# SP's queue as a fourth engine in the list that orders a hybrid-attention layer, with every transposing issue a step of its own

## The chip, the core and the metric

The kernel runs on one core of a Trainium2 chip. The metric is device time in microseconds (us): the median of several executions. The engines are called PE (matrix multiply), ACT (ScalarE), DVE (VectorE), POOL (GpSimd) and SP (SyncE, which here only issues DMAs). Every engine works through its own instructions in order. SP's instructions are DMA issues; one that waits for a semaphore holds those behind it.

## The reference

One layer, 512 tokens (`SEQ`), width 2048 (`D_MODEL`), three token mixers of 4 heads of 128, all in float32:

```python
hn = rmsnorm(x, norm_g)
proj = jnp.einsum('bsd,dc->bsc', hn, w_in)
br = proj[..., :QKVG_COLS].reshape(b, s, N_BRANCH, 4, BRANCH_W)      # q, k, v, g of three branches
f_logit = proj[..., QKVG_COLS:QKVG_COLS + N_HEADS] + b_f
gates = jax.nn.sigmoid(proj[..., QKVG_COLS + N_HEADS:] + b_gate).reshape(b, s, N_BRANCH, D_MODEL)
ya = forgetting_attention(qa, ka, va, f_logit)        # A: softmax with a cumulative forget bias, causal
yb = chunked_relpos_attention(qb, kb, vb, rel_bias)   # B: chunks of 64 and a learned relative bias
yc = stick_breaking_attention(qc, kc, vc)             # C: stick-breaking weights in log space
ys = jnp.stack([from_heads(ya), from_heads(yb), from_heads(yc)], axis=2)
ys = ys * jax.nn.silu(br[:, :, :, 3])
up = jnp.einsum('bsnw,nwd->bsnd', ys, w_up)
merged = jnp.sum(gates * up, axis=2)
return x + jnp.einsum('bsd,de->bse', merged, w_out)
```

The input projection makes 2048 -> 12,292 columns: 6,144 for q, k, v, g, 4 forget logits, and 6,144 merge gates.

## The kernel before

Float32 products are made on PE from two float32r parts each: a value is split into a high part (ACT, L249) and a low part (DVE, L253), and three products are summed (the low-low product is left out). Two columns of 128 are computed as one pair with seven products in place of eight (Strassen-Winograd), so a pair of columns is seven units. A unit has a weight tile `raw` of 512 KB, its split `w`, and 16 matmuls (L268): eight of 512 columns for the high part and eight of 256 for the low one. PE accumulates a unit in a PSUM bank; ACT (L786, L790, L807, L840) or DVE takes it out.

The order of units is written in `HEADS`: after the first head, which is computed while x is loaded, each further head brings a pair of its q and k, and the letters say what follows: `s` a pair of two heads' g, `g` a pair of merge-gate columns (24 such pairs in all, taken from one row of gates), `v` the value projection of the next branch (14 units). Between a unit's matmuls the steps of the heads are put in: norms, scores, softmax or stick-breaking, the transposing of the weights, the product with v, SiLU. Then come the `up` units (12 heads' outputs, 16 column blocks, with the gates) and the `out` units with the residual.

What comes when is settled before the chip runs, by a list: a small discrete-event plan (`Flow`). Every piece of work is a generator that yields either something to wait for (an `Event` with a planned time, free buffers in `Slots`) or `(engine, microseconds)`. The plan always takes next the step that can start first, of equal ones that with the earlier due time (ready time plus a slack: 0 for weight loads, 5 or 3 for a head's steps), and moves that engine's clock. The instruction is emitted when its step is taken. PE, ACT and DVE execute in the order of this plan (`manual_schedule`). SP's queue is not an engine of the plan: a transfer is emitted when its generator gets to it, `landing` estimates when its data are there, and only the first 48 transfers (`N_FIRST`) and those of the values are pinned to the order of emission (`keep_in_program_order`). The others may be put in another order when the program is built.

Transfers on SP: weights (`raw`), x, `xn`, fetches of what was put into DRAM (`g`, `vr`, `yr`, `sg`, `tb`, `cb`), stores (`gl` gates, `gd` a second head's g, `vd` values, `yd` heads' outputs), and transposes. Those take a head's weights of 512 x 512, causal, as ten blocks of 128 x 128: for every row block i, ACT lays the words' two halves apart (`apart`, L1230), then i + 1 transposing issues go out (L1234), and when all ten have landed, ACT puts the halves together (`together`, L1244). Before, the plan emits the i + 1 issues at once and reckons their landing aside:

```python
            turned[0] = max(turned[0], flow.fin + 0.3) + 1.3 * (i + 1)
            self.event("x", i).t = turned[0] + XLATE
```

The last head has its weights transposed on PE (`soft_trans`). The second summand of a unit's weights is added by POOL's queue (`add_up`, L286).

Of the kernel before, what the change touches and what calls it, by code (L numbers as in the profile page):

```python
# [16 lines left out]
P = 128  # L17
# [20 lines left out]
PE, ACT, DVE = 0, 1, 2  # L38
# [26 lines left out]
class Flow:  # L65
# [98 lines left out]
def hybrid_kernel(  # L164
# [106 lines left out]
    line = [0.0, 0.0]  # L271

    def landing(ready, kb):

        line[0] = max(line[0], ready) + 0.5
        line[1] = max(line[1], line[0] + 1.0) + kb / (340.0 if line[1] < 60.0 else 370.0)
        return line[1] + 1.5

    def fetch(to, src, ready, kb, queue=nc.sync, pinned=False):
        i = queue.dma_start(to, src)  # L280
        if pinned or len(first) < N_FIRST and queue is nc.sync:
            first.append(tc.keep_in_program_order(i))
        return Event(landing(ready, kb))

    def add_up(to, src, ready, kb, pinned=False):
        i = nc.gpsimd.dma_start(to, src, accum_op=ALU.add)  # L286
        if pinned:
            tc.keep_in_program_order(i)
        line[1] = max(line[1], ready + 1.0) + kb / 170.0
        return Event(line[1] + 2.5)  # L290
# [10 lines left out]
    first = [tc.keep_in_program_order(nc.sync.dma_start(begin_in, begin))]  # L301
# [76 lines left out]
    def load_unit(u):  # L378
        if isinstance(u, (Pair, VUnit)):
            if u is u.task.units[0]:  # L380
                yield from u.task.load()
            return
        for s in u.srcs:
            yield raws, 1
            t = raw_tile(u.shape)
            u.raw = t
            u.there.t = fetch(t, s, flow.ready, 4 * u.shape[0] * P * P // 1024, nc.scalar if u is units[0] else nc.sync).t
# [215 lines left out]
    class PairTask:  # L603
# [9 lines left out]
        def __init__(self, src1, src2, ops, c1_done=None, c2r_done=None, c2_done=None, late=False, rest=None,  # L613
                     x1_first=False, plain_end=False):
            self.plain_end = plain_end
            self.src, self.ops, self.late, self.rest = (*src1, *src2), ops, late, rest
            self.done = {"c1": c1_done, "c2r": c2r_done, "c2": c2_done}
            self.order = (1, 5, 2, 3, 6, 7, 4) if late else (1, 2, 6, 5, 7, 3, 4)
            if x1_first:
                self.order = (1, 5, 6, 2, 7, 3, 4)  # L620
            self.w, self.there, self.ps = {}, {p: Event() for p in range(1, 8)}, {}
            self.ev = {p: Event() for p in range(1, 8)}
            self.r, self.r_ev, self.c2_ev = None, Event(), Event()
            self.bank, self.pools, self.tile = {}, accs, acc
            self.units = [Pair(self, i) for i in range(7)]
# [4 lines left out]
        def load(self):  # L630
            a11, a12, a21, a22 = self.src
            for p, srcs in ((5, (a21, a22)), (1, (a11,)), (2, (a12,)), (7, (a11, a21)), (4, (a22,))):
                yield raws, 1
                t = self.w[p] = raw_tile()
                ev = fetch(t, srcs[0], flow.ready, 512)
# [71 lines left out]
        def after_of(self, i):  # L707
# [68 lines left out]
            def go():  # L776
# [31 lines left out]
                elif p == 7:  # L808
# [10 lines left out]
                    yield from fold(self.c2[:, RH], self.v)  # L819
                    give(t2s)  # L820
# [10 lines left out]
                else:  # L831
# [11 lines left out]
                    give(bank)  # L843
                    finished("c2", self.c2)
# [27 lines left out]
    class ValueTask:  # L872
# [19 lines left out]
        def keep(self, g, s):  # L892

            def go(c):
                yield rstd_ev
                for i, h in enumerate((LH, RH)):
                    yield ACT, act_us(HS)
                    nc.scalar.activation(c[:, h], c[:, h], AF.Copy, scale=rcol[:, 2 * i + s:2 * i + s + 1])
                nc.sync.dma_start(self.dram[g][s], c)
                t = landing(flow.fin, 256)  # L900
                t2s.free.append(t)
                self.kept[g][s].t = t
            return go
# [4 lines left out]
        def load(self):  # L908
# [3 lines left out]
            def begin(p, kh, queue):  # L912
# [6 lines left out]
                for to, c in pieces(p, kh):  # L919
                    ev = fetch(to, src({5: 2, 1: 0, 2: 1, 7: 0, 4: 3}[p], kh)[:, c], flow.ready,  # L920
                               128 * (c.stop - c.start), queue, True)
# [93 lines left out]
    def forget_bias():  # L1015
# [6 lines left out]
        nc.sync.dma_start(parts, fd.rearrange("(n h) (c t) -> n (h c) t", h=NH, t=T).rearrange("n c t -> c n t"))  # L1022
# [23 lines left out]
        nc.sync.dma_start(fd2.rearrange("h (c t) -> (h c) t", t=T), v)  # L1046
# [11 lines left out]
    turned = [0.0]  # L1058

    class Head:  # L1060
# [93 lines left out]
        def soft_start(self):  # L1154
# [3 lines left out]
            if n == A:  # L1158
                yield f2_ev
                self.bias = t2("cb")  # L1160
                nc.sync.dma_start(self.bias, fd2[self.h:self.h + 1, :].partition_broadcast(P))
                yield Event(landing(flow.now, 256))
# [4 lines left out]
            else:  # L1167
                self.bias = t2("tb")
                ev = fetch(self.bias, rel[self.h], flow.now, 256)
# [44 lines left out]
        def apart(self, i):  # L1214
# [18 lines left out]
            for j in range(i + 1):  # L1233
                nc.sync.dma_start_transpose(out=self.tt[j][:, :, (i - j) * P:(i - j + 1) * P],  # L1234
                                            in_=u[:, 2 * j * P:2 * (j + 1) * P])
# [76 lines left out]
        def value(self):  # L1312
# [9 lines left out]
            for s in range(2):  # L1322
                ev = fetch(to[:, :, s, :], task.dram[g][s].rearrange("p (i h d) -> p i h d", i=2, h=2)[:, :, d, :],
                           flow.now, 128)
# [6 lines left out]
        def silu(self):  # L1331

            if (self.n, self.h) in gd:
# [4 lines left out]
                yield fetch(g, d, flow.now, 256)  # L1338
# [22 lines left out]
        def av(self):  # L1361
# [48 lines left out]
    def spill(n, d, c):  # L1410
        gl[n, d] = dp.tile([P, S], F32, name=nm("gl"))
        nc.sync.dma_start(gl[n, d], c)
        stored(t2s, 1, 256)

    def gate_units(late=False, x1_first=False):
        n, d = gates.pop(0)

        def keep(i):
            def go(c):
                yield from by_norm(c)  # L1420
                spill(n, d + i, c)
# [4 lines left out]
    def far(n, h):  # L1426
# [3 lines left out]
        def go(c):  # L1430
            yield from by_norm(c)
            nc.sync.dma_start(d, c)
            ev.t = landing(flow.fin, 256)
# [3 lines left out]
    def first_quad(head):  # L1437
# [57 lines left out]
        def take_f():  # L1495
# [5 lines left out]
            for j in range(NQ):  # L1501
                nc.sync.dma_start(fd[NH * j:NH * (j + 1), :], v[32 * j:32 * j + NH, :])
# [67 lines left out]
    def split_y(i):  # L1570
        def go():
# [4 lines left out]
            else:  # L1576
                yield t2s, 1
                t = t2("yr")
                yield fetch(t, yd[n, h], flow.now, 256)
# [11 lines left out]
    def gates_of(d):  # L1591
        evs = []
        for n in (C, B, A):
            yield t2s, 1
            sig[n, d] = t2("sg")
            evs.append(fetch(sig[n, d], gl[n, d], flow.now, 256))
# [115 lines left out]
    def out_pair(e):  # L1712
# [3 lines left out]
        def rest(task):  # L1716
            yield t2s, 2
            for i in range(2):
                r[i] = t2("xr")
                ev = fetch(r[i], xT[e + i], flow.now, 256)  # L1720
# [35 lines left out]
    def loads():  # L1756
        def x(kt):
# [5 lines left out]
            x_in[kt].t = fetch(xraw[kt], xT[kt], 0.0, 256).t  # L1763

        def n(i):
            yield t2s, 1
            t = t2("xn")
            n_in[i].t = fetch(t, xn[i // NQ, i % NQ], 0.0, 256).t
# [44 lines left out]
    line[:] = 0.8, 1.9  # L1813
# [29 lines left out]
N_FIRST = 48  # L1843
# [53 lines left out]
```

## Time and profile before

| | |
|---|---|
| median of 3 runs | 1307.88 us (1307.13 to 1309.7) |
| the profiled execution's own time | 1307.3 us |
| its span, first to last instruction | 1305.6 us |
| mean granted PE clock | 0.999 |
| busy: PE, PE weight load, DVE, ACT | 1294.0, 1128.8, 1144.7, 883.8 us |
| transposing issues on SP | 110 |

The profile is of one execution. Rows of busy time by stretch read: the stretch in us from the start and its length, then for PE, PE's weight load, DVE, ACT and POOL the busy us with the number of instructions, then the granted PE clock (1.00 is full), the mean busy share of the 16 DMA engines and GB/s. Rows of waits read: engine, tile and line that waited, what ended the wait; us in total, times, the longest. Rows of the timeline read: start, length, engine, line, operation, out<-in, count, and in brackets how long the engine had been idle and what ended it; neighbours of one kind are merged, so a length on SP (SPq) runs from the first issue's start to the last one's end. A PE row that is merged takes in small pauses.

### The profile page before, as it was taken

Reading aid. Unit: us, or ns where it says so; the run is one execution under the profiler, and the core shown is the slowest. Engines: PE = TensorE matmul, PEld = TensorE weight load, DVE = VectorE, ACT = ScalarE, POOL = GpSimd, SP = SyncE. Lnnn points to the kernel's source line nnn. Section 1 sums busy time; section 2 is a strip of 40 time slices with the busy share of each in tenths; the row PEclk is TensorE's granted clock in tenths of the full one; section 3 lists DMA queues with packets and bytes.
Section 4 is the critical chain, followed back from the end, with each engine's and each line's share of the span. In section 5 each row is a group of like instructions: output and inputs, shape, how many; then the busy total and the mean of one; then the engine's idle time right before and its main releaser. Section 6 shows DMA issues by size and latency. Waiting matters only on the chain.

```text
span 1305.6 us, 20205 instructions
## 1 busy us (share of the span) xinstructions
PE 1294.0 (99%) x7247; PEld 1128.8 (86%) x7247; DVE 1144.7 (88%) x1693; ACT 883.8 (68%) x1380; POOL 106.8 (8%) x138
## 2 busy tenths in 40 slices
PE   9999999999999999999999999999999999999998
PEld 6888888888888888888888888888888888898887
DVE  8989989888898999989869989999898888898786
ACT  8887677767867768667767767776857655454443
POOL 0200100020010000101100001001010000001000
PEclk9999999999999999999999999999999999999999
DMA  9879797878789878886888669898789765778883
GB/s 340 238 190 253 175 237 203 219 201 209 219 211 225 227 201 218 211 236 174 213 217 218 183 184 256 180 254 195 214 224 298 259 194 169 205 180 251 236 239 110
DMA packets 132420, 282.90 MB, mean 217 GB/s; under 512 B 43344, under 2 KB 51536, under 8 KB 132320
## 3 DMA queue, kind: packets, MB, share of 16 engines
q1 hardware_dynamic: 111200, 217.32, 52.1%
q0 software_dynamic: 17376, 59.78, 26.8%
q10 hardware_dynamic: 3744, 4.52, 1.0%
q8 instruction: 57, 0.93, 0.3%
q14 instruction: 43, 0.35, 0.1%
HBM read 249.92 MB, written 24.42 MB: 210 GB/s over the span
## 4 chain that ended last, share of the span: by engine, by line
PE 85%; DVE 5%; DMA 5%; ACT 3%; issue 1%; SPq 0%; ACTq 0%; POOL 0%; DVEq 0%; POOLq 0%
PE acc L268 71%; PE att L268 10%; DMA raw<-in_w_col 3%; DVE w L253 2%; ACT w L249 1%; DMA raw<-in_w_v 1%; PE att L264 1%; PE att L265 1%; PE att L263 1%; PE att L1372 1%; PE att L1373 1%; PE att L1371 0%; DMA g<-gd 0%; SPq L1234 0%; ACT p L1244 0%
## 5 line engine op out<-in xcount | busy, mean ns | idle before, releaser
L253 DVE TENSOR_TENSOR w<-raw,w 128x1024 fp32r<-128x1024 f32 (+2 forms) x424 | 499.8, 1184 | 109.4 <-ACT w L249 107.7
L249 ACT ACTIVATE w<-raw 128x1024 fp32r<-128x1024 f32 (+2 forms) x424 | 434.5, 1026 | 212.2 <-PE acc L268 84.5
L268 PE MATMUL acc<-x,w 128*128 128x512 f32 (+1 forms) x2656 | 500.1, 339 | 1.6 <-ACT v L790 1.0
L268 PEld LDWEIGHTS acc<-x,w 128*128 128x128 f32 x2656 | 425.1, 190 | 68.2 <-issue 3.0
L268 PE MATMUL acc<-t,w 128*128 128x256 f32 (+1 forms) x1920 | 360.7, 339 | 4.6 <-ACT u L807 3.2
L268 PEld LDWEIGHTS acc<-t,w 128*128 128x128 f32 x1920 | 293.4, 191 | 40.2 <-ACT u L807 3.8
L268 PE MATMUL acc<-m,w 128*128 128x256 f32 (+1 forms) x960 | 157.3, 326 | 0.3 <-DVE m L253 0.3
L268 PEld LDWEIGHTS acc<-m,w 128*128 128x128 f32 x960 | 141.4, 190 | 16.3 <-DVE m L253 0.5
L286 POOL DMA_DIRECT2D raw<-in_w_col x80 | 69.0, 863 | 783.3 <-DMA raw<-in_w_col 263.1
L268 PE MATMUL att<-y,w 128*128 128x512 f32 x384 | 89.7, 389 | 0.0
L268 PEld LDWEIGHTS att<-y,w 128*128 128x128 f32 x384 | 72.1, 188 | 14.9
L268 PE MATMUL acc<-w,x 128*128 128x512 f32 (+1 forms) x336 | 62.9, 338 | 0.6 <-DVE w L253 0.6
L647 DVE TENSOR_TENSOR raw<-raw,raw 128x1024 f32<-128x1024 f32 x48 | 58.6, 1220 | 0.3
L268 PEld LDWEIGHTS acc<-w,x 128*128 128x128 f32 x336 | 52.1, 190 | 7.6 <-DVE w L253 1.0
L653 DVE TENSOR_TENSOR raw<-raw,raw 128x1024 f32<-128x1024 f32 x48 | 58.5, 1219 | 0.1
L786 ACT ACTIVATE u<-acc 128x512 f32<-128x512 f32 x50 | 29.8, 595 | 39.6 <-PE acc L268 34.6
L807 ACT ACTIVATE u<-acc 128x512 f32<-128x512 f32 x49 | 29.0, 592 | 39.2 <-PE acc L268 38.8
L527 DVE TENSOR_TENSOR c<-c,begin_in 128x512 f32<-128x512 f32 x80 | 54.1, 685 | 0.1
L790 ACT ACTIVATE v<-acc 128x512 f32<-128x512 f32 x53 | 31.4, 593 | 28.4 <-PE acc L268 28.2
L726 DVE TENSOR_TENSOR c<-u 128x256 f32<-128x256 f32 x105 | 44.1, 424 | 2.8
L268 PE MATMUL acc<-y,w 128*128 128x512 f32 x192 | 46.1, 389 | 0.0
L840 ACT ACTIVATE c<-acc 128x256 f32<-128x256 f32 x49 | 18.5, 378 | 40.1 <-PE acc L268 32.5
(216 smaller groups left out, 1356.8 us busy)
## 6 DMA issues: line engine op xcount, KB each, us to landing
raw<-in_w_col SPq DMA_DIRECT2D x200, 512.0 KB, 4.8
raw<-in_w_col POOLq DMA_DIRECT2D x80, 512.0 KB, 7.1
raw<-in_w_out SPq DMA_DIRECT2D x40, 512.0 KB, 4.7
raw<-in_w_v SPq DMA_DIRECT2D x24, 512.0 KB, 5.6
gl<-c SPq DMA_DIRECT2D x48, 256.0 KB, 5.3
raw<-in_w_up SPq DMA_DIRECT2D x32, 384.0 KB, 3.3
sg<-gl SPq DMA_DIRECT2D x48, 256.0 KB, 4.6
raw<-in_w_out POOLq DMA_DIRECT2D x16, 512.0 KB, 6.8
```

What stands on the lines that cost most here:

```text
L249: nc.scalar.activation(hi, src, AF.Copy)
L253: nc.vector.tensor_sub(lo, src, f(hi))
L268: nc.tensor.matmul(ps, w, x, start=start, stop=stop, skip_group_check=more)
L286: i = nc.gpsimd.dma_start(to, src, accum_op=ALU.add)
L527: nc.vector.tensor_mul(c, c if src is None else src, rstd[0][:c.shape[0], :])
L647: nc.vector.tensor_add(w[1], w[1], w[5])
L653: nc.vector.tensor_add(w[2], w[2], w[1])
L726: add(to, src[:, LH], src[:, RH])
L786: nc.scalar.activation(self.u, ps, AF.Copy)
L790: nc.scalar.activation(self.v, ps, AF.Copy)
L807: nc.scalar.activation(self.s, ps, AF.Copy)
L840: nc.scalar.activation(c, ps[:, RH], AF.Copy, scale=-1.0)
```

## The change

SP becomes the fourth engine of the plan. Every transfer that SP issues is a step on it, 0.4 us for a plain one and 1.28 us for a transposing one, emitted when the step is taken, and pinned to that order. `landing` is reckoned from the step's end. `XLATE`, the plan's time from the last transposing issue to the data, is 4 where it was 8 on top of its own reckoning. `HEADS` places the 24 gate pairs anew. A planned event `right_ev` makes the pair's last step wait for the right half's. `N_FIRST` goes.

```diff
-PE, ACT, DVE = 0, 1, 2
+PE, ACT, DVE, SP = 0, 1, 2, 3
...
-    LATE = (0.3, 0.12, 0.12)
+    LATE = (0.3, 0.12, 0.12, 0.0)
...
-        self.clock = [0.0] * 3
-        self.idle = [0.0] * 3
+        self.clock = [0.0] * 4
+        self.idle = [0.0] * 4
...
-    def landing(ready, kb):
-
-        line[0] = max(line[0], ready) + 0.5
-        line[1] = max(line[1], line[0] + 1.0) + kb / (340.0 if line[1] < 60.0 else 370.0)
-        return line[1] + 1.5
-
-    def fetch(to, src, ready, kb, queue=nc.sync, pinned=False):
-        i = queue.dma_start(to, src)
-        if pinned or len(first) < N_FIRST and queue is nc.sync:
-            first.append(tc.keep_in_program_order(i))
-        return Event(landing(ready, kb))
+    def landing(issued, kb):
+
+        line[0] = max(line[0], issued + 1.0) + kb / (340.0 if line[0] < 60.0 else 370.0)
+        return line[0] + 1.5
+
+    def queued(dma, to, src, us=0.4):
+
+        yield SP, us
+        tc.keep_in_program_order(dma(to, src))
+
+    def fetch(to, src, kb):
+        yield from queued(nc.sync.dma_start, to, src)
+        return Event(landing(flow.fin, kb))
+
+    def store(to, src, kb):
+        yield from queued(nc.sync.dma_start, to, src)
+        return landing(flow.fin, kb)
...
                     yield from fold(self.c2[:, RH], self.v)
+                    set_(self.right_ev)
...
                     give(bank)
+                    yield self.right_ev
                     finished("c2", self.c2)
...
             for j in range(i + 1):
-                nc.sync.dma_start_transpose(out=self.tt[j][:, :, (i - j) * P:(i - j + 1) * P],
-                                            in_=u[:, 2 * j * P:2 * (j + 1) * P])
-            turned[0] = max(turned[0], flow.fin + 0.3) + 1.3 * (i + 1)
-            self.event("x", i).t = turned[0] + XLATE
+                yield from queued(nc.sync.dma_start_transpose, self.tt[j][:, :, (i - j) * P:(i - j + 1) * P],
+                                  u[:, 2 * j * P:2 * (j + 1) * P], 1.28)
+            self.event("x", i).t = flow.fin + XLATE
...
-                nc.sync.dma_start(yd[self.n, self.h], self.y)
-                stored(t2s, 1, 256)
+                t2s.free.append((yield from store(yd[self.n, self.h], self.y, 256)))
...
-        nc.sync.dma_start(gl[n, d], c)
-        stored(t2s, 1, 256)
+        t2s.free.append((yield from store(gl[n, d], c, 256)))
...
-    line[:] = 0.8, 1.9
+    line[0], flow.clock[SP] = 1.9, 0.8
...
-XLATE = 8.0
+XLATE = 4.0
...
-HEADS = [(C, 1, "g"), (C, 2, "sgg"), (C, 3, "v"), (B, 0, "sggg"), (B, 1, "gg"), (B, 2, "sggg"), (B, 3, "gv"), (A, 0, "s"), (A, 1, "ggg"), (A, 2, "sggg"), (A, 3, "ggggg")]
+HEADS = [(C, 1, "gg"), (C, 2, "sg"), (C, 3, "v"), (B, 0, "sggg"), (B, 1, "g"), (B, 2, "sggg"),
+         (B, 3, "gvg"), (A, 0, "sgg"), (A, 1, "gg"), (A, 2, "sggg"), (A, 3, "gggg")]
...
-N_FIRST = 48
```

All other calls of `fetch` and of SP's `dma_start` become `yield from fetch(...)`, `store(...)` or `queued(...)` in the same way.

More of the change, by code (lines that the diff above doesn't have):

```diff
@@ L386, in load_unit @@
             u.raw = t
-            u.there.t = fetch(t, s, flow.ready, 4 * u.shape[0] * P * P // 1024, nc.scalar if u is units[0] else nc.sync).t
+            kb = 4 * u.shape[0] * P * P // 1024
+            if u is units[0]:
+                nc.scalar.dma_start(t, s)
+                u.there.t = landing(flow.ready, kb)
+            else:
+                u.there.t = (yield from fetch(t, s, kb)).t
     def prep(u):
@@ L919, in begin @@
                 for to, c in pieces(p, kh):
-                    ev = fetch(to, src({5: 2, 1: 0, 2: 1, 7: 0, 4: 3}[p], kh)[:, c], flow.ready,
-                               128 * (c.stop - c.start), queue, True)
+                    w, kb = src({5: 2, 1: 0, 2: 1, 7: 0, 4: 3}[p], kh)[:, c], 128 * (c.stop - c.start)
+                    if queue is nc.sync:
+                        ev = yield from fetch(to, w, kb)
+                    else:
+                        tc.keep_in_program_order(queue.dma_start(to, w))
+                        ev = Event(landing(flow.ready + 0.5, kb))
                 self.there[p, kh].t = ev.t
@@ L1337, in silu @@
                 g = t2("g")
-                yield fetch(g, d, flow.now, 256)
+                yield (yield from fetch(g, d, 256))
             else:
@@ L1578, in go @@
                 t = t2("yr")
-                yield fetch(t, yd[n, h], flow.now, 256)
+                yield (yield from fetch(t, yd[n, h], 256))
             yield xps, 1
```

45 lines of the change are left out of this document (21 added, 24 removed).

## The prediction

> **What bounds the kernel now.** I read the page's engine line first, then busy time in stretches of 50 us, then who waited for whom on PE and on ACT, and last the timeline around the places where PE stood still.
>
> ```profile
> span 1305.6 us, 20205 instructions
> PE 1294.0 (99%) x7247; PEld 1128.8 (86%) x7247; DVE 1144.7 (88%) x1693; ACT 883.8 (68%) x1380; POOL 106.8 (8%) x138
> ...
> 0.00:50.00 50.00, 48.94 (x226) 36.04 (x227) 44.84 (x96) 42.55 (x94) 2.53 (x13) 1.00 0.90 317
> 100.00:150.00 50.00, 50.00 (x295) 44.47 (x294) 44.85 (x72) 33.41 (x49) 3.46 (x4) 1.00 0.86 232
> 300.00:350.00 50.00, 48.84 (x276) 42.33 (x275) 41.61 (x51) 38.01 (x59) 4.31 (x5) 1.00 0.80 212
> 600.00:650.00 50.00, 49.42 (x283) 43.31 (x283) 43.78 (x73) 36.10 (x59) 9.10 (x12) 1.00 0.77 200
> 650.00:700.00 50.00, 48.19 (x269) 42.15 (x268) 38.93 (x50) 35.31 (x55) 4.31 (x5) 0.97 0.81 214
> 750.00:800.00 50.00, 47.61 (x270) 40.96 (x269) 41.62 (x60) 34.66 (x55) 3.45 (x4) 1.00 0.79 221
> 850.00:900.00 50.00, 49.60 (x290) 43.89 (x289) 45.19 (x61) 28.91 (x41) 4.00 (x5) 1.00 0.93 245
> 900.00:950.00 50.00, 49.53 (x283) 43.15 (x282) 45.98 (x72) 41.38 (x67) 4.33 (x5) 1.00 0.78 202
> 1000.00:1050.00 50.00, 50.00 (x242) 42.22 (x241) 43.50 (x67) 34.57 (x53) 0.00 (x0) 1.00 0.74 253
> 1150.00:1200.00 50.00, 49.67 (x322) 45.33 (x321) 41.74 (x57) 24.15 (x29) 4.32 (x5) 1.00 0.83 222
> ```
>
> PE is busy for 1294.0 of 1305.6 us, so all its idle time is 11.6 us, and no change of order can bring much more than that. The rows above are the stretches with idle PE (the rest read 50.00, as 100 to 150 and 1000 to 1050 do). The 1.06 us of the first is the start. In the middle there are 1.16 us at 300, 0.58 at 600, 1.81 at 650, 2.39 at 750, 0.40 at 850, 0.47 at 900 and 0.33 at 1150. At 650 the granted clock also falls to 0.97. Who ended these waits:
>
> ```profile
> PE acc L268 <- ACT u L807: 3.2, 3, 1.8
> PE acc L268 <- DVE w L253: 1.8, 3, 0.7
> ...
> ACT w L249 <- DMA raw<-in_w_col: 30.8, 12, 5.1
> ACT y L1347 <- DMA g<-gd: 4.4, 1, 4.4
> ```
>
> PE names ACT and DVE, but ACT itself had waited on transfers: 30.8 us for weights and 4.4 us for one `g`. ACT runs in order, so whatever stands behind its waiting instruction is late too, and L807, which empties PE's accumulator, is one of those. The timeline tells why the transfers were late. The worst place:
>
> ```profile
> 653.64 5.05 SPq L1234 DMA_TRANSPOSE tt<-p  x4
> 658.74 0.58 SPq L280 DMA_DIRECT2D g<-gd  x1
> 664.95 0.63 ACT L1347 ACTIVATE y<-g 128x512 f32<-128x512 f32 x1 [4.40 <-DMA g<-gd]
> 666.14 0.58 ACT L807 ACTIVATE u<-acc 128x512 f32<-128x512 f32 x1
> 666.78 3.64 PE L268 MATMUL acc<-t,w 128*128 128x256 f32 x14 [1.81 <-ACT u L807]
> 668.09 1.35 ACT L1244 ACTIVATE p<-tt 128x1024 uint16<-128x1024 uint16 x1
> ```
>
> SP's queue is in the middle of four transposing issues from 653.64 to 658.69; only then does it issue `g`, which lands at 664.9. ACT sits on `y<-g` for 4.40 us, L807 stands behind it, and PE gets its bank at 666.78. The second and third places are the same with weights in the part of `g`:
>
> ```profile
> 768.73 6.34 SPq L1234 DMA_TRANSPOSE tt<-p  x5
> 777.08 1.94 SPq L280 DMA_DIRECT2D raw<-in_w_col  x4
> 779.14 1.06 ACT L249 ACTIVATE w<-raw 128x1024 fp32r<-128x1024 f32 x1 [5.07 <-DMA raw<-in_w_col]
> 783.96 3.06 PE L268 MATMUL acc<-x,w 128*128 128x512 f32 x16 [0.62 <-ACT w L249]
> 793.69 3.06 PE L268 MATMUL acc<-t,w 128*128 128x512 f32 x16 [1.02 <-ACT u L807]
> 786.45 3.25 ACT L1244 ACTIVATE p<-tt 128x1024 uint16<-128x1024 uint16 x4
> ...
> 312.85 5.59 SPq L1234 DMA_TRANSPOSE tt<-z  x4
> 318.55 1.94 SPq L280 DMA_DIRECT2D raw<-in_w_col  x4
> 322.57 1.06 ACT L249 ACTIVATE w<-raw 128x1024 fp32r<-128x1024 f32 x1 [4.39 <-DMA raw<-in_w_col]
> 337.38 2.82 PE L268 MATMUL acc<-x,w 128*128 128x512 f32 x14 [1.01 <-ACT v L790]
> ```
>
> Four to six transposes go out in one block, the `raw` loads follow behind it, ACT waits 5.07 and 4.39 us for them, and PE stops within the next 5 to 15 us. So the kernel is bound by PE everywhere, and of what it loses in the middle most goes back to one cause: SP was taken up by transposing issues of which the kernel's list knew nothing.
>
> **The change part by part.** *Each transposing issue becomes a step of 1.28 us on SP.* The price in the list against the chip:
>
> ```profile
> L1234 SPq DMA_TRANSPOSE tt<-p x46: 1173/1237/2699, 403.4 to 922.2; - x46
> DMA to landing us min/median/max: 2.3/3.7/8.5
> ```
>
> The median issue is 1.24 us, so the 1.28 is right to 4%. The number of issues, of transfers and of bytes stays as it is; what moves is their order. A head's ten transposes come in blocks of one to four from one ACT copy each, and until now a block was put in the list without a pause. As steps they compete for SP: where both are ready the earlier due time goes first. A load has slack 0, a head's step 5, so loads get in between two transposes and wait for 1.24 us, not for a block of 5 to 6; a `g` fetch, with slack 5 itself, gets in once it was ready before the next transpose of the row. The list also knows now when a `g` or a weight can have landed and puts ACT's instruction on it later, behind the emptying of PE's banks.
>
> What that can give back, from the rows above: idle PE of 1.16 (300), 1.81 (650), 2.39 (750), 0.40 and 0.47 (850, 900) is 6.23 us; the 0.58 at 600 ends on DVE's `w` and I leave it out, likewise the 0.33 at 1150, long after the last transpose. Besides there is the clock after the stop at 666:
>
> ```profile
> 665.00:666.70 1.70, 0.00 (x0) 0.00 (x0) 0.00 (x0) 1.67 (x4) 0.00 (x0) 1.00 1.05 357
> 666.70:670.00 3.30, 3.22 (x14) 2.77 (x15) 1.83 (x2) 3.30 (x6) 0.00 (x0) 0.70 1.03 414
> 670.00:675.00 5.00, 5.00 (x24) 4.16 (x24) 2.97 (x5) 4.87 (x7) 0.86 (x1) 0.86 0.89 224
> ```
>
> 0.30 of 3.3 us and 0.14 of 5 us are 0.99 and 0.70, together 1.69 us of PE work that the stop cost on top of its idle time. So 7.9 us hang on SP's order. [...]
>
> How much of it comes back I take stretch by stretch. At 650 the cause is one fetch behind one block, and both are steps now: 3.0 of 1.81 + 1.69. At 750 weights, ACT's copies and DVE's work come together, and interleaving makes the loads only 3 to 4 us earlier of the 5.07 that ACT waited: 1.6 of 2.39. At 300: 0.8 of 1.16. At 850 to 950: 0.4 of 0.87. The sum is 5.8 us. It could be all 7.9, or nothing if the loads are held by something else.
>
> *All SP transfers are pinned.* The first 48 and the values' loads were pinned already, so the first 60 us keep their order (0, at most 0.5 either way). Behind them the queue was free to be issued in another order than the list's; it now issues the list's own. Stores (`gl`, `yd`, `vd`, `gd`) and fetches (`vr`, `yr`, `sg`) take their place by the planned time of their data. A pinned transfer that waits holds everything behind it: weights, transposes, then ACT and PE. What SP waits for now:
>
> ```profile
> SPq L280 <- DVE w L253: 496.4, 202, 12.9
> SPq L1412 <- DVE c L527: 86.7, 26, 8.4
> ```
>
> The long one is, as I read it, SP waiting for a free weight buffer with nothing urgent behind; the stores already wait 86.7 us in 26 places, up to 8.4, without a stop of PE that goes back to them. The trace has no wait of the new kind, so bounds: 0 from these stores, and the 666 event from above, 1.81 + 1.69 = 3.5 us, if a store holds a load for as long as the block did. I take one small stop of the size of the one at 783.96 (0.6) and round up to 1.0, since the list is right to within a few per cent for SP, nearer to the stores. In the last third (`up` and `out`) the order of `sg` against weights changes most; PE there reads 50.00, with no idle time to win and a price of about 0.3 (the row at 1150) if a load is late.
>
> *XLATE from 8 to 4.* The list lets ACT read the transposed tiles 4 us after SP's last issue. Now the copies come at 668.09 and 786.45, about 9.5 us after the blocks ended (658.69 and 776.97). Landing takes 3.7 us from an issue's start, 2.5 from its end, at most 8.5 or 7.3. At the median, 4 is enough, and the softmax chain of a head gets some 4 us shorter; nobody on PE waits for that (0). At the maximum ACT would wait 3.3 us with PE's banks behind it; the waits of 4.4 to 5.1 above cost PE 0.6 to 3.5. I take 0 here and keep that for a rival.
>
> *Gate units placed anew.* There are 24 gate pairs before and after, so PE's work does not change. A unit is 16 matmuls:
>
> ```profile
> 1158.53 143.71 PE acc L268 x849
> ```
>
> 143.71 / 849 x 16 = 2.71 us, a gate pair 7 units or 19 us. Head A0, the one at 650, goes from 14 to 28 units; B3 and C1 gain 7 each; C2, B1, A1 and A3 lose 7 each. This thins out the work of ACT, DVE and SP where PE stopped (A0), and packs it in B1 (14 units). C1 has 14 units now in the row at 100 and PE reads 50.00 there; A0 has 14 and is the worst. So B1 lies between 0 and 3.5; I take 0, because B1 like C1 has no value units just before it. A0's gain is in the 3.0 above. `right_ev` adds no wait on the chip that the data did not have: 0.
>
> **The sum.** 5.8 back, 1.0 lost: 4.8 us. The profiled execution took 1307.3 us (span 1305.6); it would take 1302.5. The median of the three runs, 1307.88, lies 0.58 above it, so I forecast 1303.1. A difference of 0.2%, 2.6 us, is about what can be told from no change here.
>
> **The rivals.** *A pinned wait takes the block's place (slower).* The list is a forecast. Where a store's data come later on the chip than planned, SP stands still, the loads behind it come late, and PE stops with a clock drop: 3.5 us an event. One event eats most of the sum, two give 5.8 - 7.0, 1.2 slower; three, of eleven heads with transposes and 24 gate pairs with two stores each, give 4.7 slower, 1312.6. It decides from the third event on. For it: 496.4 us of waiting on SP, with 12.9 the longest. Against: the stores' waits cost PE nothing now, and ACT and DVE have been in the list's order all along. Chance 0.24.
>
> *The early copies wait (same).* If the transposes of half of the eleven heads land late enough to cost PE the 0.6 of the 783.96 stop, 3.3 us go back: 4.8 - 3.3 = 1.5 faster, 1306.4. For it: the 8.5 us maximum. Against: the 2.5 at the median. Chance 0.09.
>
> *Issue time does not matter (same).* If the loads are late because transfers share the DMA engines, or the queue had nearly this order, the stops only move: 1307.9. For it: the DMA share is 0.79 to 0.86 in most rows above. Against: `g` lands 6.2 us after its issue, and 5.05 more went by before that. Chance 0.07. [...]
>
> **How the numbers follow.** The forecast has 0.60. Its own range runs from 1299.4 (7.9 and the 0.58 at 600 come back, nothing lost) to 1305.3 (2.6 are left). The range goes from 1298.9, where the start gives its 0.5 as well, to 1312.6: it takes in both rivals without a gain and the slower one up to its third event. The chances: faster by over 0.2% is the forecast, 0.60; the two rivals near zero give 0.16 for within 0.2%; the pinned wait gives 0.24 for slower.
>
> **What would show it.** Right: on SP loads stand between single transposes, with no block of four ahead of a load; ACT's wait for `raw<-in_w_col` falls from 30.8 to below 20, and the 4.4 for `g<-gd` is gone; PE idles 5 to 8 us in all, and the clock stays at 1.00 in every stretch of 50 us. Wrong: PE's idle time stays above 11, a new large wait on SP at a store (L1412's successor) or ACT waiting for `tt`, or a stretch with the clock below 0.98 at B1, A1 or A2.

## The result and the profile after

| | before | after |
|---|---|---|
| median of 6 runs, us | 1307.76 (1307.1 to 1309.7) | 1298.47 (1298.2 to 1300.57) |
| ratio, 95% interval | | 0.9932 [0.9919, 0.9945] |
| the profiled execution, us | 1307.3 | 1298.3 |
| its span, us | 1305.6 | 1296.5 |

The change made the kernel 9.3 us faster. The forecast was 4.8 us, and its range began 0.4 us above the median that came out: the direction was right, the size was half.

The engine line of the page after:

```profile
span 1296.5 us, 20194 instructions
PE 1289.8 (99%) x7247; PEld 1127.6 (87%) x7247; DVE 1148.6 (89%) x1693; ACT 884.3 (68%) x1380; POOL 106.9 (8%) x138
```

PE's idle time fell from 11.6 to 6.7 us, by 4.9. PE's busy time fell as well, by 4.2 us, though the number of matmuls, 7247, is the same. Busy time by stretch after (stretch and length, then PE, weight load, DVE, ACT, POOL, then clock, DMA share, GB/s):

```profile
0.00:50.00 50.00, 48.19 (x226) 35.61 (x227) 44.85 (x97) 43.04 (x95) 2.54 (x13) 1.00 0.89 319
50.00:100.00 50.00, 49.52 (x276) 42.87 (x275) 45.88 (x71) 40.48 (x80) 8.34 (x11) 1.00 0.78 190
100.00:150.00 50.00, 49.65 (x287) 43.54 (x286) 44.69 (x72) 31.92 (x46) 4.32 (x5) 1.00 0.90 227
...
300.00:350.00 50.00, 50.00 (x289) 44.21 (x288) 44.69 (x57) 39.93 (x62) 4.31 (x5) 1.00 0.87 217
...
600.00:650.00 50.00, 50.00 (x293) 44.41 (x292) 41.57 (x67) 37.41 (x63) 4.48 (x7) 1.00 0.86 213
650.00:700.00 50.00, 50.00 (x290) 44.27 (x290) 46.04 (x59) 36.20 (x52) 5.03 (x6) 1.00 0.87 215
...
750.00:800.00 50.00, 50.00 (x289) 44.17 (x288) 48.04 (x65) 35.77 (x53) 5.19 (x6) 1.00 0.83 216
...
850.00:900.00 50.00, 50.00 (x289) 44.27 (x288) 47.60 (x76) 32.78 (x52) 4.32 (x5) 1.00 0.83 218
900.00:950.00 50.00, 49.57 (x286) 43.71 (x285) 44.57 (x58) 35.17 (x52) 4.32 (x5) 1.00 0.95 213
...
1100.00:1150.00 50.00, 49.68 (x273) 43.30 (x272) 44.30 (x68) 26.70 (x40) 2.59 (x3) 1.00 0.67 191
```

All idle time is gone at 300, 600, 650, 750 and 850, and the clock reads 1.00 in each of these stretches, also at 650. What is left in the middle is 0.43 us at 900. The start got worse: 0.75 us more idle time in the first stretch, 0.48 and 0.35 in the next two, 1.58 in all. Who waited, on PE (us in total, times, longest):

```profile
PE acc L268 <- ACT w L408: 0.7, 1, 0.7
PE acc L268 <- DVE w L253: 0.7, 2, 0.5
PE att L1118 <- DVE sq L253: 0.4, 1, 0.4
```

and on ACT:

```profile
ACT w L249 <- DMA raw<-in_w_col: 1.7, 1, 1.7
ACT p L1258 <- DMA tt<-p: 4.3, 2, 2.6
ACT sg L1613 <- DMA sg<-gl: 16.4, 13, 2.2
```

ACT's wait for weights went from 30.8 us in 12 places to 1.7 in one, and the 4.4 for `g<-gd` is gone from the list. Two waits are there instead, 4.3 us for transposed tiles (L1258 is the old L1244) and 16.4 us for `sg` in the `up` stage, and L818, the old L807, is not among PE's releasers. Both waits for tiles lie between 700 and 930 us, a stretch in which PE waits for nothing; whether its wait of 0.43 us at 930.9 (for DVE's `sq`) goes back to the second of them, which ended at 917.2, is open. At head A0, where PE had stood still for 1.81 us, the timeline now reads (SP's issues and the two instructions of ACT that had been late):

```profile
639.20 0.53 SPq L281 DMA_DIRECT2D raw<-in_w_col  x1
639.82 1.18 SPq L281 DMA_TRANSPOSE tt<-u  x1
640.47 0.63 ACT L1361 ACTIVATE y<-g 128x512 f32<-128x512 f32 x1
641.10 0.52 SPq L281 DMA_DIRECT2D raw<-in_w_col  x1
641.72 1.17 SPq L281 DMA_TRANSPOSE tt<-u  x1
643.00 0.53 SPq L281 DMA_DIRECT2D raw<-in_w_col  x1
643.62 5.08 SPq L281 DMA_TRANSPOSE tt<-p  x3
648.82 0.50 SPq L281 DMA_DIRECT2D raw<-in_w_col  x1
649.42 2.50 SPq L281 DMA_TRANSPOSE tt<-p  x2
...
653.34 3.48 SPq L281 DMA_TRANSPOSE tt<-p  x2
...
657.03 1.37 ACT L1258 ACTIVATE p<-tt 128x1024 uint16<-128x1024 uint16 x1
```

Between two `raw` loads go one to three transposes, and L1361 (`y<-g`, before L1347) starts with no bracket behind it, that is, without a wait. The first copy of transposed tiles starts at 657.03, 0.2 us after the last transposing issue ended (653.34 + 3.48); before it came 9.4 us after.

### The profile page after: what moved, and what is told of

It reads as the page before. It is cut to its first block, busy times and chain, and to the rows that moved or that the text cites. A ratio compares the mean times of both kernels' runs of the same rounds, so it can differ in the third digit from the quotient of the medians.

```text
span 1296.5 us, 20194 instructions
## 1 busy us (share of the span) xinstructions
PE 1289.8 (99%) x7247; PEld 1127.6 (87%) x7247; DVE 1148.6 (89%) x1693; ACT 884.3 (68%) x1380; POOL 106.9 (8%) x138
## 4 chain that ended last, share of the span: by engine, by line
PE 92%; DVE 4%; DMA 1%; issue 1%; ACT 1%; SPq 1%; DVEq 0%; ACTq 0%
PE acc L268 77%; PE att L268 10%; DVE w L253 2%; PE att L1386 1%; PE att L1387 1%; PE att L264 1%; PE att L265 1%; SPq L281 1%; PE att L263 1%; PE att L1385 1%; DVE m L253 0%; DMA tt<-p 0%; DMA lf_parts<-fd 0%; DMA gl<-c 0%; DVE c L538 0%
## 5 line engine op out<-in xcount | busy, mean ns | idle before, releaser
L268 PE MATMUL acc<-x,w 128*128 128x512 f32 (+1 forms) x2656 | 497.2, 339 | 0.7 <-ACT w L408 0.7
L268 PEld LDWEIGHTS acc<-x,w 128*128 128x128 f32 x2656 | 426.0, 189 | 66.5 <-issue 2.5
L268 PE MATMUL acc<-t,w 128*128 128x512 f32 (+1 forms) x1920 | 358.7, 338 | 0.4 <-DVE w L253 0.3
L268 PEld LDWEIGHTS acc<-t,w 128*128 128x128 f32 x1920 | 291.5, 190 | 33.3 <-ACT vh L249 0.4
L268 PE MATMUL acc<-m,w 128*128 128x256 f32 (+1 forms) x960 | 157.3, 327 | 0.3 <-DVE m L253 0.3
L268 PEld LDWEIGHTS acc<-m,w 128*128 128x128 f32 x960 | 141.4, 190 | 16.3 <-DVE m L253 0.5
L268 PE MATMUL att<-y,w 128*128 128x512 f32 x384 | 89.6, 389 | 0.0
L268 PEld LDWEIGHTS att<-y,w 128*128 128x128 f32 x384 | 72.1, 188 | 14.9
L268 PE MATMUL acc<-w,x 128*128 128x512 f32 (+1 forms) x336 | 63.8, 339 | 0.0
L818 ACT ACTIVATE u<-acc 128x512 f32<-128x512 f32 x49 | 29.1, 594 | 46.5 <-PE acc L268 44.2
L268 PEld LDWEIGHTS acc<-w,x 128*128 128x128 f32 x336 | 52.2, 190 | 7.1 <-issue 0.4
L268 PE MATMUL acc<-y,w 128*128 128x512 f32 x192 | 46.1, 389 | 0.0
```

What stands on the lines that cost most here:

```text
L268: nc.tensor.matmul(ps, w, x, start=start, stop=stop, skip_group_check=more)
L818: nc.scalar.activation(self.s, ps, AF.Copy)
```

## The experiments

All times below are medians in us; the ratios are against the kernel before on the same chip, with 95% intervals. Its median on these chips lay between 1306.8 and 1307.8, so the ratios compare better than the times. "Changed" is the kernel after, "before" the kernel before, each with one edit.

**Is it SP's issue time?** The first kernel keeps the list of before word for word and makes the chip's issue cheaper: a plain copy of each block takes the place of its transposing (the weights are then not transposed).

```diff
-                nc.sync.dma_start_transpose(out=self.tt[j][...], in_=u[:, 2 * j * P:2 * (j + 1) * P])
+                nc.sync.dma_start(self.tt[j][...], u[:, 2 * j * P:2 * (j + 1) * P].rearrange("p (h c) -> p h c", h=2))
```

> The kernel before with each transposing issue replaced by a plain copy of the same bytes (the transposing is left out, the rest of the work stays). A plain issue takes about 0.33 us on SP where a transposing one takes 1.24. If the transposes' issue time is what makes loads late: ACT's 30.8 us for raw<-in_w_col fall below 12, the stops at 666 and 784 go, 1299 to 1304. If transfers on shared DMA engines are the cause: 1306 to 1309 with the same waits.

1297.98, ratio 0.9931 [0.9917, 0.9944]. The issues at L1234 (minimum, median, maximum in ns) and their landing:

```profile
L1234 SPq DMA_DIRECT2D tt<-p x46: 488/614/1772, 400.9 to 906.7; - x46
DMA to landing us min/median/max: 2.0/4.0/8.7
```

and ACT's wait for weights:

```profile
ACT w L249 <- DMA raw<-in_w_col: 0.4, 1, 0.4
```

and PE's largest wait behind the start:

```profile
PE acc L268 <- DVE w L253: 0.7, 1, 0.7
```

The issue's median falls from 1.237 to 0.614 us; the landing does not get quicker (median 4.0 against 3.7), nor does that of the `raw<-in_w_col` loads once they are issued (5.0 against 4.8). ACT's wait for weights falls from 30.8 to 0.4 us, the stops at 337, 666, 784 and 793 are gone, PE's idle time falls from 11.6 to 5.7 us, and the time by 0.7%, just what the change brought (and 1 us more than the expectation gave). PE, ACT, DVE and POOL go through the same instructions in the same order in both traces, so no reshuffled list has a part in this. SP's queue, not all of it pinned, differs in 14 of 646 places. Most swap a load with a neighbour, but one matters: `g` now goes out at 647.18, ahead of the four copies of its block, where it had stood behind them. So the stop at 666 may owe its end to that order as well as to the shorter issues. At 300 and 750, where the weights were late, no load moves ahead of a block. There it was the time that the issues held SP, and not the transfers themselves, that made the loads late. The same edit in the changed kernel, with its list and its price of 1.28 left as they are:

> The changed kernel, its list and price of 1.28 as they are, with each transposing issue replaced by a plain copy of the same bytes (the transposing is left out), which takes 0.6 us on SP. In the kernel before the same edit gave 8.8 us. If the changed list has already put all of the transposes' issue time where nobody waits: 1296.5 to 1298.5. If half of it is still in PE's way: 1292 to 1295.

1297.14, 0.9925 [0.9912, 0.9939]. The interval overlaps that of the change itself. Once the list counts the issues, taking half their time away brings 1.3 us by the medians and 0.9 by the ratios. That also bounds what the other kind of transfer is worth by itself, beside the issue.

**Which part of the change does it?** Two constants changed along with the list's new engine. They were put back in the changed kernel and put into the kernel before:

```diff
a_oldheads  -HEADS = [(C, 1, "gg"), (C, 2, "sg"), ...]     +HEADS of before          (changed)
a_xlate8    -XLATE = 4.0                                   +XLATE = 8.0              (changed)
b_newheads  -HEADS = [(C, 1, "g"), (C, 2, "sgg"), ...]     +HEADS of the changed     (before)
b_xlate4    -XLATE = 8.0                                   +XLATE = 4.0              (before)
b_new4      both constants of the changed kernel                                     (before)
```

> The changed kernel with the gate pairs where they stood before (the old HEADS); SP stays an engine of the list. Theory 'queue' (the gain comes from the list knowing what an issue costs on SP): most of the 9.3 us stays, 1299 to 1302. Theory 'gates' (the gain comes from moving gate pairs away from the crowded places): 1305 to 1308, with PE idle again near head A0 (650 to 700).

> The kernel before with the new HEADS alone. Theory 'queue': 1305 to 1309, ACT still waits some 20 to 30 us for raw<-in_w_col. Theory 'gates': 1299 to 1302.

> The changed kernel with XLATE 8 again. Theory 'queue': 4 us more of slack cost or give little, 1298 to 1300, and ACT's 4.3 us of waiting for tt go. Rival 'early copies' (the shorter way through a head is part of the gain): 1301 to 1304.

> The kernel before with XLATE 4 alone. Theory 'true list': 1304 to 1312; the list's landing times leave out SP's waiting, and ACT waits longer for tt and raw. Rival 'short head' (4 us less in each head's way is a gain by itself): 1300 to 1303.

> The kernel before with both new constants, the new HEADS and XLATE 4, but SP no engine of the list and the queue pinned as before. Theory 'true list' (the constants help only a list that knows SP's time): 1305 to 1313, ACT waits 15 us or more for raw<-in_w_col. Rival 'constants' (HEADS and XLATE together are the gain): 1298 to 1301.

| HEADS, XLATE | SP not in the list | SP in the list, each issue a step, pinned |
|---|---|---|
| old, 8 | 1307.8 (before) | not run |
| old, 4 | 1331.45, 1.0182 [1.0159, 1.0205] | 1306.72, 0.9995 [0.9986, 1.0004] |
| new, 8 | 1316.95, 1.0074 [1.0061, 1.0088] | 1321.59, 1.0103 [1.0087, 1.0118] |
| new, 4 | 1307.89, 1.0006 [0.9996, 1.0016] | 1298.47, 0.9932 [0.9919, 0.9945] |

The constants without the new engine bring nothing (1307.89), and the new engine between the same new constants brings 9.4 us. But the gain is not the engine's alone: with the old HEADS the changed kernel is as slow as before. ("XLATE" is not quite one quantity in the two columns, since the old list adds it to a reckoning of its own.) Three of the five expectations missed on the slow side, with both of their theories: b_newheads (1316.95), a_xlate8 (1321.59) and b_xlate4 (1331.45). a_oldheads came out in the range of 'gates', but not with the stops that this theory named: 650 to 700 reads 50.00 there. What goes on in the cells shows in their waits. In the kernel before with both new constants, ACT's wait for weights:

```profile
ACT w L249 <- DMA raw<-in_w_col: 34.6, 15, 5.0
```

and the stretches:

```profile
300.00:350.00 50.00, 48.43 (x279) 42.43 (x279) 42.28 (x55) 38.53 (x60) 4.31 (x5) 1.00 0.85 226
400.00:450.00 50.00, 48.12 (x268) 42.25 (x266) 39.83 (x51) 32.15 (x47) 4.32 (x5) 0.97 0.80 223
```

The old cause is all there: 34.6 us of ACT's waiting, 1.57 us idle at 300, and at 400, the place of B1 with 14 units, 1.88 us idle and the clock at 0.97. The changed kernel reads 50.00 at both. Now the changed kernel with the old HEADS, PE's waits:

```profile
PE acc L268 <- DVE w L253: 3.3, 5, 2.0
PE acc L268 <- ACT u L818: 1.5, 2, 1.2
PE att L1118 <- DVE sq L253: 1.4, 1, 1.4
```

the stretches with the most idle time:

```profile
750.00:800.00 50.00, 48.82 (x282) 42.92 (x281) 45.19 (x67) 36.20 (x55) 5.19 (x6) 1.00 0.96 231
800.00:850.00 50.00, 48.12 (x276) 42.25 (x275) 46.11 (x77) 36.86 (x60) 3.46 (x4) 1.00 0.74 185
850.00:900.00 50.00, 47.73 (x276) 41.88 (x276) 43.36 (x58) 27.59 (x40) 3.47 (x5) 1.00 0.83 232
```

and ACT's wait for weights:

```profile
ACT w L249 <- DMA raw<-in_w_col: 1.4, 1, 1.4
```

Here the cause is cured (1.4 us of waiting for weights, against 30.8), and PE stops all the same: 5.3 us between 750 and 900, with DVE's splits and ACT's L818 as the largest releasers. So a true list cures the loads, and with this placing of the gate units the other engines' order does not hold. With XLATE 8 in the changed kernel, PE's waits:

```profile
PE acc L268 <- DVE w L253: 5.2, 6, 1.9
PE att L1386 <- DVE vl L253: 3.3, 4, 1.4
PE att L1385 <- ACT vh L249: 2.5, 1, 2.5
```

and a stretch:

```profile
1000.00:1050.00 50.00, 45.87 (x224) 38.36 (x223) 40.27 (x65) 32.59 (x55) 0.00 (x0) 0.93 0.69 227
```

No wait for `raw<-in_w_col` is left on ACT. 5.8 us of the stops are in the heads' product with v (L1385, L1386), which stands later in the list; for the last transposed head it falls at 1028.7, in the `up` stage. About as much stands behind DVE's splits, 3.1 us of it at 250 to 300, and what ties these to XLATE was not found.

Is A0, the head of the worst stop, the place that HEADS mends? The changed kernel with the old HEADS but for A0, A1 and A3:

```diff
-HEADS = [(C, 1, "gg"), (C, 2, "sg"), ..., (B, 1, "g"), ..., (B, 3, "gvg"), (A, 0, "sgg"), (A, 1, "gg"), ..., (A, 3, "gggg")]
+HEADS = [(C, 1, "g"), (C, 2, "sgg"), ..., (B, 1, "gg"), ..., (B, 3, "gv"), (A, 0, "sgg"), (A, 1, "gg"), ..., (A, 3, "gggg")]
```

> The changed kernel with the old HEADS but for head A0, which gets its two gate pairs (one from A1, one from A3). The prediction's step: A0 is the crowded place and its pairs carry what HEADS gives, 1298 to 1302. Rival: all places together make it, 1303 to 1309.

1306.31, 0.9998 [0.9986, 1.0009]: no gain over the old HEADS (1306.72). The units at A0, A1 and A3 do not carry it by themselves (or the list that they make loses it again elsewhere: 750 to 800, 850 to 900 and 950 to 1000 have 1.5 to 2.1 us idle each).

How much does such a constant move the time by itself? Two small steps, one in each kernel:

```diff
b_plus    -XLATE = 8.0   +XLATE = 8.3   (before)
a_xlate5  -XLATE = 4.0   +XLATE = 5.0   (changed)
```

> The kernel before with XLATE 8.3 in place of 8.0, a change that by itself means nothing: a measure of how far any small change of the list moves the time. If single changes can be read by themselves: 1306 to 1309. If the list's order hangs on every tenth of a us, so that a set of constants fits only the list it was found with: 1310 to 1320.

> The changed kernel with XLATE 5. If 4 leaves ACT waiting for late transposes (4.3 us in the changed kernel's trace) and 5 is still short enough for the heads: 1296.5 to 1298.5 with that wait below 2 us. If the time rises evenly from XLATE 4 to 8, where it was 1321.6: about 1304.

b_plus: 1311.77, 1.0033 [1.0021, 1.0046]. An edit of 0.3 us in a planned time, which says nothing new of the chip, costs 4 to 5 us: a reshuffled list can do as much by itself, and a difference of that size between two cells of the table proves no mechanism. It is one such step and no upper bound. The 9.4 and 8.2 us of the last row and column are about twice that, so they rest on the waits beside them more than on their size. a_xlate5: 1298.43, 0.9934 [0.9922, 0.9946], the same as the change. So the changed kernel does not stand on one value of XLATE alone. With 5 ACT's 4.3 us of waiting for `tt<-p` are gone and the time is the same, so that wait cost PE little or nothing.

**One step for each issue, the pins, the price.** The block of a row as one step; the pins taken from what had none before; the pins alone, in the kernel before; and the price of an issue too low and too high:

```diff
a_block     -for j in range(i + 1): yield from queued(dma_start_transpose, ..., 1.28)
            +yield SP, 1.28 * (i + 1)
            +for j in range(i + 1): tc.keep_in_program_order(nc.sync.dma_start_transpose(...))
a_unpinned  queued pins only the first 48 transfers and the values' loads
b_pinned    every nc.sync.dma_start... of before inside tc.keep_in_program_order(...)
a_cheap     -..., 1.28)   +..., 0.4)
a_dear      -..., 1.28)   +..., 1.6)
```

> The changed kernel with a row's i + 1 transposing issues as one step of 1.28 (i + 1) us on SP, so that no load gets between them. If knowing the time is what counts: 1298 to 1302. If getting loads between the transposes is what counts, as the prediction had it: 1303 to 1308, with ACT's wait for raw<-in_w_col over 10 us again.

1303.89, 0.9976 [0.9967, 0.9985]: 5.4 us of the gain are lost again by the medians, 5.8 by the ratios. ACT's wait for weights:

```profile
ACT w L249 <- DMA raw<-in_w_col: 9.7, 8, 2.9
```

PE's largest wait:

```profile
PE acc L268 <- ACT u L818: 2.2, 1, 2.2
```

and the worst stretch:

```profile
500.00:550.00 50.00, 47.83 (x271) 42.27 (x270) 43.96 (x72) 33.89 (x54) 4.33 (x5) 0.97 0.82 230
```

The wait for weights is back at 9.7 us in 8 places, near the 10 that the prediction's theory asked for. The longest, of 2.9 us, ends at 756.3 behind a block, and PE stops for 1.20 us at 766.9, released by ACT: that is the old picture. The worst stop is not. It ends at 523.0, and between 490 and 550 ACT waits for no transfer at all; until L818's turn comes it is at work on other steps, or waits for PE and DVE. With that, and with a loss not much above b_plus's, it is likely but not shown that knowing the time is not enough and loads must get in between.

> The changed kernel, SP still an engine of the list, but only the first 48 transfers and the values' loads pinned, as before; the rest may be put in another order. Theory 'queue': the list's times do the work, 1298 to 1301. Rival 'pins' (the gain comes from holding the order): 1304 to 1308.

> The kernel before with every SP transfer pinned to the order in which it is written, and SP still no engine of the list. Theory 'true list': 1305 to 1310. Rival 'pins': 1299 to 1302. The prediction's rival of a pinned wait in the block's place would be 1309 to 1314.

a_unpinned: 1298.77, 0.9931 [0.9918, 0.9944]. b_pinned: 1310.18, 1.0027 [1.0014, 1.004]. In the changed kernel the pins bring and cost nothing. In the kernel before they cost about 3.5 us. ACT's waits for weights and `sg` there:

```profile
ACT w L249 <- DMA raw<-in_w_col: 28.7, 12, 5.2
ACT sg L1602 <- DMA sg<-gl: 18.3, 20, 2.7
```

and the stretch that lost most against the kernel before:

```profile
100.00:150.00 50.00, 47.17 (x264) 41.24 (x263) 42.59 (x69) 30.17 (x43) 3.93 (x5) 0.97 0.86 212
```

The loads are nearly as late as before (28.7 against 30.8), `sg` is waited for in 20 places, and 100 to 150, which read 50.00 before, has 2.83 us of idle time. Its cause stands just ahead of it on DVE:

```profile
107.39 0.26 DVE L1026 TENSOR_REDUCE lf<-lf_parts 128x16 f32<-128x64 f32 x1 [4.56 <-DMA lf_parts<-fd]
```

The small fetch of `lf_parts` goes out at 104.64, pinned behind three transposing issues; DVE stands still for it, and PE gets its split weights at 109.10. In the kernel before, L1026 starts at 102.70 without a wait.

> The changed kernel with 0.4 us as the list's price of a transposing issue, that of a plain one, where the chip takes 1.2. Every issue is still a step and pinned. Theory 'true list' (the right price is what counts): 1302 to 1308, and ACT waits 10 us or more for transfers again. Rival 'order is enough' (steps by due time, whatever their price): 1298 to 1301.

1341.73, 1.0266 [1.0249, 1.0283], the slowest of all. ACT's waits for the transposed tiles:

```profile
ACT p L1258 <- DMA tt<-p: 26.3, 10, 6.8
ACT z L1258 <- DMA tt<-z: 9.9, 4, 5.1
```

and a stretch:

```profile
100.00:150.00 50.00, 43.14 (x237) 37.61 (x236) 38.21 (x63) 27.52 (x40) 4.32 (x5) 0.93 0.80 200
```

36.2 us of waiting for tiles that the list believed landed long ago, and 6.86 us idle in the one stretch, with the clock at 0.93.

> The changed kernel with 1.6 us as the list's price of a transposing issue, where the chip takes 1.2. Theory 'true price' (a wrong price costs on either side; here the list delays heads that could go on, with no wait for transfers): 1302 to 1315, ACT waiting under 3 us for tt and raw<-in_w_col. Rival 'slack' (any generous price does): 1297 to 1300.

1317.32, 1.0076 [1.006, 1.0092], outside both ranges. This one is not conclusive. ACT waits 1.3 us for tiles and not at all for `raw<-in_w_col`; PE's largest wait is for DVE's splits, 7.3 us in 6 places.

Too high a price as such does no harm, as a_plain shows: there the list reckons 1.28 for an issue that the chip does in 0.60 (the median of the copies of `tt<-p`), and the time is the best of all. So a_dear seems slow because of the order that the list makes with 1.6, not because it is untrue; why that order is worse was not found.

## Why the prediction was half right

*What bounds the kernel.* Right. The cause that it read from the waits and the timeline, transposing issues on SP of which the list knew nothing, is shown by b_plain, for the stop at 666 with the order of one fetch beside it. Two cures for it come to the same time: the issue made cheaper on the chip (1297.98) and the list told of it (1298.47).

*What can come back: the step that failed.* By the same rows as in the sum, before against after:

| stretch | forecast | measured |
|---|---|---|
| 300 | 0.8 | 1.16 |
| 600 | left out | 0.58 |
| 650, with the clock | 3.0 | 3.50 |
| 750 | 1.6 | 2.39 |
| 850 to 950 | 0.4 | 0.44 |
| sum | 5.8 | 8.07 |
| start, 0 to 150 | 0 | -1.58 |
| waits behind pinned transfers | -1.0 | none found |
| PE's busy time besides the clock | not thought of | 2.5 |
| total | 4.8 | 9.0 |

The span fell by 9.1. The step that failed is the one that takes stretch by stretch how much of the loss comes back: it took 5.8 of 7.9 us, and 8.07 came. In all, four terms were mis-sized. First, these shares: nearly all of the loss came back, where I took about three quarters and left out 600 because DVE ended its wait there; that stop is gone too. Second, the 1.0 for a pinned transfer that waits was not lost: a_unpinned gives the same time.

Third, the start has 1.58 us more idle time, where I had taken 0 and at most 0.5. Of this, 0.75 lies in the first 50 us and is no loss: PE does 226 matmuls there before and after, and other kernels whose list is the same up to there read 48.93 (a_xlate5, a_plain), as before did with 48.94. The 0.48 of the next stretch belongs to the new list: 50 to 100 reads 49.50 to 49.54 in every kernel that has it and 50.00 in every one that has not.

Last, I took PE's idle time and the clock for the whole loss. PE's busy time fell by 4.2, and the clock is 1.69 of that; 2.5 us of loss had stood as busy time. Most of it shows in the starts of the matmuls. Behind the first 60 us and outside the stretch at half clock (0.50 from 668.1 to 671.3 in the trace of before), 23 matmuls before start over 80 ns later than the median distance for the shape ahead of them, 10.1 us too late in all; after, there are 11, 3.0 us too late. Of these times PE is drawn idle for 7.15 and 1.58. So 1.5 of the 2.5 us is delay that the matmul ahead of a stop covers: one of L268 is drawn 339 ns long on average, but 2656 of them take 497.2 us, one in 187 ns. Another 0.75 is that of the first 50 us, idle time in one trace and busy time in the other.

*Each transposing issue as a step of 1.28.* Right in mechanism: the issues' time made the loads late (b_plain), loads now go between the transposes (the timeline above), and the price is right to a few per cent:

```profile
L281 SPq DMA_TRANSPOSE tt<-p x46: 1172/1196/2612, 391.6 to 911.5; - x46
```

How much of the gain hangs on the single steps, a_block leaves open. A price of 0.4, too low, costs 43 us. The issue is a third of the time to landing here, 1.24 us of 3.7 (before), and halving it (0.61, with a landing of 4.0, in b_plain) was worth 0.69% [0.56, 0.83].

*XLATE and the gate units at 0.* Wrong for each by itself, and hidden by their being changed together. Here the right direction was in part luck: the forecast's gain hung on SP's steps and needed neither constant, yet with the old HEADS these steps bring nothing (1306.72). XLATE 4 was costed by who waits for the tiles; put back to 8 it costs 23 us. HEADS was costed by how full each head is; the old one costs 8.2. Both move every later step of the list, and b_plus shows how far the time moves with a list that has merely been shuffled. I know of no reading of the trace of before that would have given these two; the forecast should have said so with a wider range on the gain's side. That the constants fit only the list they were found with would explain the table, but is argued, not shown. The place that I had in mind for HEADS, A0, does not bring the gain alone (a_onlya0); B1 with 14 units lost 1.88 us under the old kind of list (b_new4), with the clock of its row at 0.97, as in that of the stop at 666, where the clock cost 1.69; with as much here, an estimate, it is 3.6 in all and so at the upper end of the 0 to 3.5 that I gave it, and nothing under the new.

*The rivals.* A pinned wait in the block's place: not found here (a_unpinned gives the same time, and SP's waits for stores hardly moved), though pinning held up a fetch in the list of before (b_pinned). Early copies that wait: ACT waits 4.3 us for tiles, at next to no cost (a_xlate5). Issue time that does not matter: refuted (b_plain); the DMA share of 0.79 to 0.86 that spoke for it stands in only five of the ten rows shown.

*The markers.* As forecast: the wait for `raw` below 20 (1.7), the `g` wait gone, 5 to 8 us idle (6.7), clock 1.00 at B1, A1 and A2. One block of four transposes is left, at 175.3, ahead of a store. Of the signs of failure one came, ACT waiting for `tt` (4.3 us), without the failure that it was to mean.

*What stays open.* Which places of HEADS carry the 8.2 us; what the new engine gives with the old HEADS and XLATE 8; how much of the gain the single steps bring over a block of known length; why the new list stops PE at 50 to 150; and why 1.6 makes so bad an order. No version beat the changed kernel: a_xlate5 is equal to it, and a_plain leaves out the transposing.

## What to carry to other kernels

Where a list settles the order of the work, every queue that takes time must stand in it with its measured price, also one that only issues transfers; a wait for a load is then followed back to what its queue was doing before the issue. Long issues are best put in one by one, so that urgent loads get in between; here a block of known length kept only part of the gain, though not all of that difference is shown to come from the loads. Constants found with one list are no neutral ground for another: move them a little as a control (0.3 us cost 4 to 5 us here), and test a change of the list with both sets before its gain or loss is put down to the change.

## What the runs showed of the hardware

A transposing issue holds SP for 1.24 us (before) and a plain copy of the same block for 0.61 (b_plain), with landings of 3.7 and 4.0 us at the median: in these runs the price of the transposing lies in the issue, not in the transfer.

A longer stop was not always followed by a lower clock. Two stops of PE, in the changed kernel with the old HEADS:

```profile
852.86 1.22 PE L268 MATMUL acc<-t,w 128*128 128x256 f32 x8 [1.95 <-DVE w L253]
```

and with the blocks:

```profile
523.00 4.62 PE L268 MATMUL acc<-t,w 128*128 128x256 f32 x16 [2.17 <-ACT u L818]
```

After the first, of 1.95 us, eight matmuls of 256 columns take 1.22 us (0.15 each), and the row 850 above has the clock at 1.00. After the second, of 2.17 us, sixteen take 4.62 (0.29 each), where sixteen at 532.15 in the same trace take 2.96, and the clock of its stretch is 0.97. In the kernel before, a stop of 1.81 us was followed by a clock of 0.70 over the next 3.3 us. In b_new4 the stretch from 400 to 450, with 1.88 us idle, reads 0.97. So a stop of 1.95 us left the clock at 1.00 and a shorter one did not; what decides it these runs do not show.
